# A decoder block's first 26 microseconds: who casts the weights, what is loaded first, and how long TensorE is warmed

## The chip, the cores and the metric

The kernel runs on one core of one Trainium2 chip. The metric is the device time of one execution in microseconds (us). The engines are TensorE (PE in the profile; its weight loads are PEld), VectorE (DVE), ScalarE (ACT), GpSimd (POOL) and SyncE (SP, which here issues most of the DMAs).

## The reference

One layer of a hybrid block on 512 rows of 1024 channels, all in float32. The part that bears on the change is its beginning, the first normalisation and the input projection:

```python
h = rmsnorm(x, norm1_g[l])
z = h @ w_in[l] + b_in[l]                       # 1024 -> 6656 columns
z_glu, z_rx, z_rg, z_ga, z_gb = jnp.split(z, split_idx, axis=-1)
u = z_glu[..., :D_CONV] * jax.nn.sigmoid(z_glu[..., D_CONV:])
...                                             # depthwise convolution, layernorm, silu, projection
...                                             # 4-tap convolution, RG-LRU with block-diagonal gates, projection
m = jax.nn.sigmoid(z_ga) * y_a + jax.nn.sigmoid(z_gb) * y_b
x = x + m @ w_mix_out[l]
h = rmsnorm(x, norm2_g[l])
x = x + (jax.nn.silu(h @ ffn_w1[l]) * (h @ ffn_w3[l])) @ ffn_w2[l]
return rmsnorm(x, norm_f_g)
```

## The kernel before

**How a product is made.** Every float32 operand of a matmul is split in two float32r parts: a high part, which is a cast of the full value, and a low part, the full value minus the high one. `mm3` adds three products per tile of 128 channels: high by high, high (weights) by low (rows), low (weights) by high (rows). With `lo_last=True` all products with the weights' high part come first and those with its low part at the end.

**Weight chunks.** The weights of the projection come in chunks of 1024 x 128 (512 KB), one for each 128 output columns. `emit_chunk` (L140) issues the load on SyncE's queue (L156) into one of `RAW = 4` buffers `raw_in`, and `split_to` (L120) makes the high part `hl_in` with `copy` (L122, on ScalarE, `act.copy`) and the low part on GpSimd (L118, a subtraction of two inputs of 128x1024). `emit_to(n)` emits chunks until n of them are out.

**Small parameters.** Biases, gains and convolution taps are loaded as rows of 128 into tiles `rows` by `load_rows` (L463), one DMA for each of the `parts`, and turned on TensorE into columns by `rows_turned` (L498), from where VectorE copies them into `par` (L499). `row_at` says in which tile and row a parameter lies. Before, norm1_g (8 rows) and b_in (52) share the first tile and are the `first` two parts, the other rows lie in three more tiles.

**The beginning, in an order written out by hand** (L586 to L609, for TensorE, ScalarE, VectorE and SyncE):

- `WARM` float32 matmuls of ones (L486) run on TensorE ahead of everything; each shows as two records in the trace.
- The 512 rows of x lie in four tiles of 128 rows, each in two halves of 512 columns. `norm1_rows(t)` computes two sums of squares on ScalarE (L530, L536) and a square root (L537), a statistic and a reciprocal on VectorE (L531, L538), and scales the rows in place on VectorE (L570).
- `turn_half` turns 256 rows: for each of the 8 blocks of 128 channels two transposes on TensorE (L554), the high part `h1*h` on ScalarE (L557) and the low part `h1*l` on VectorE (L558). The transposes of the second half need banks that the low parts of earlier blocks free.
- `early_mm(i, hf)` multiplies half `hf` of the rows with early chunk i, 24 matmuls of 256 columns (L514). TensorE's order is: warming, first rows turned, first half turned, `early_mm(0, 0)`, `early_mm(1, 0)`, second half turned, `early_mm(2, 0)`, `early_mm(3, 0)`, remaining rows turned, `early_mm(i, 1)` for i = 0 to 3.

SyncE's order before is: x of the first two row tiles, norm1_g, b_in, chunks 0 and 1, x of the last two row tiles, chunk 2, thirteen loads of small rows, chunk 3. After this beginning a planner orders the rest of the kernel (GpSimd's part as well).

Of the kernel before, what the change touches and what calls it, by code (L numbers as in the profile page):

```python
# [13 lines left out]
P = 128  # L14
# [12 lines left out]
ND = D // P  # L27
# [6 lines left out]
RAW = 4  # L34
HL = 5
AHEAD = 4
WARM = 12

FEW, MANY = 32, 112

# [12 lines left out]
ROWS = [  # L53
    ("norm1_g", 8), ("b_in", 52), ("conv_dw_b", 8), ("conv_ln_g", 8), ("conv_ln_b", 8),
    ("conv_b_out", 8), ("lru_conv_b", 10), ("lru_ba", 10), ("lru_bx", 10),
    ("lru_lambda", 10), ("norm2_g", 8), ("lru_conv_w", 40),
    ("conv_dw_w", 248),
]
# [27 lines left out]
def tile_block(ctx, tc, a, out):  # L86
# [15 lines left out]
    def pairt(name, dtype=F32R):  # L102

        return longt(f"{name}h", dtype), longt(f"{name}l", dtype)

    def bank(name):
        return psum.tile([P, T], F32, tag="mm", name=name)

    def bank2(name):
        return psum2.tile([P, T], F32, tag="cv", name=name)  # L110

    vec, act, pe, pool_e = nc.vector, nc.scalar, nc.tensor, nc.gpsimd
# [4 lines left out]
    def sub(eng, o, x, y):  # L117
        return eng.tensor_tensor(out=o, in0=x, in1=y, op=ALU.subtract)  # L118

    def split_to(h, l, full, eng, copy=act.copy):  # L120

        copy(h, full)  # L122
        last = sub(eng, l, full, h.bitcast(F32))
        if eng is pool_e:
            newest["sub"] = last.ins
        return h, l
# [10 lines left out]
    def wchunk(key, src, kt, cols, where="hl", lo=pool_e, after=None):  # L137
        chunks.append((key, src, kt, cols, where, lo, after))

    def emit_chunk():  # L140
        if emitted[0] == GATES_AT:
            load_gates()
        key, src, kt, cols, where, lo, after = chunks[emitted[0]]
        emitted[0] += 1
        n = kt * cols
        if where == "made":
            raw = src()
        else:
            raw = raws.tile([P, 1024], F32, tag="raw", name=f"raw_{key}")
        rv = raw[:, :n]  # L150
        if where == "made":
            pass
        elif callable(src):
            src(raw)
        else:
            newest["load"] = nc.sync.dma_start(rv.rearrange("p (k n) -> p k n", k=kt), src).ins  # L156
        if where != "long":
            hl = hls.tile([P, 2, 1024], F32R, tag="hl", name=f"hl_{key}")
            h, l = split_to(hl[:, 0, :n], hl[:, 1, :n], rv, lo)
            if after:  # L160
                after(rv, h)
            held[key] = (h.rearrange("p (k n) -> p k n", k=kt), l.rearrange("p (k n) -> p k n", k=kt))
        else:
            held[key] = [
                split_to(longt(f"{key}h{i}", F32R), longt(f"{key}l{i}", F32R), rv[:, i * T : (i + 1) * T], lo)
                for i in range(2)
            ]

    def emit_to(n):
        while emitted[0] < min(len(chunks), n):  # L170
            emit_chunk()

    def weights(key, ahead=AHEAD):
        i = next(i for i, c in enumerate(chunks) if c[0] == key)
        emit_to(i + 1 + ahead)
        return held.pop(key)
# [16 lines left out]
    def load_gates():  # L193
      with tc.issue_after(newest["load"]):
        for gi, name in enumerate(("lru_wa", "lru_wx")):
            nc.sync.dma_start(gate_rows[:, gi, :], a[name][0].rearrange("h r n -> (h r) n"))
# [246 lines left out]
    n_rows = sum(n for _, n in ROWS)  # L443
    n_first = ROWS[0][1] + ROWS[1][1]
    par = consts.tile([P, n_rows], F32, name="par")
    row_at = lambda c: (0, c) if c < n_first else (1 + (c - n_first) // P, (c - n_first) % P)
    at, col, parts = 0, {}, []
    for name, n in ROWS:
        col[name] = at
# [10 lines left out]
    def load_rows(i):  # L460
        lo, m, src = parts[i]
        b, r = row_at(lo)
        nc.sync.dma_start(rowt[b][r : r + m, :P], src)  # L463

    x_nat = a["x"].rearrange("b (t p) d -> p (b t) d", p=P)
    xt = [[longt(f"x{t}{h}") for h in range(2)] for t in range(NT)]

    def load_x(t):
        for h in range(2):
            nc.sync.dma_start(xt[t][h], x_nat[:, t, h * T : (h + 1) * T])  # L470
# [13 lines left out]
    wp = bank2("warm")  # L484
    for _ in range(WARM):
        pe.matmul(wp[:, :P], ones, ones, start=True, stop=True)  # L486

    first = [i for i, (lo, _, _) in enumerate(parts) if lo < n_first]
    load_x(0)
    load_x(1)  # L490
    for i in first:
        load_rows(i)

    def rows_turned(c0, c1):
        pt = bank2(f"par_ps{c0}")
        for c in range(c0, c1, P):
            m = min(P, c1 - c)
            pe.transpose(pt[:, c - c0 : c - c0 + m], rowt[row_at(c)[0]][:m, :P], ident[:m, :m])  # L498
        vec.tensor_copy(par[:, c0:c1], pt[:, : c1 - c0])  # L499

    def pc(name, i):
        return par[:, col[name] + i : col[name] + i + 1]


    def mm3(ps, ws, xs, lo_last=False):


        n = 3 * len(ws)
        i = 0
        three = [((wh, xh), (wh, xl), (wl, xh)) for (wh, wl), (xh, xl) in zip(ws, xs)]  # L510
        if lo_last:
            three = [q[:2] for q in three] + [q[2:] for q in three]
        for l, r in (q for qs in three for q in qs):
            pe.matmul(ps, l, r, start=i == 0, stop=i == n - 1)  # L514
            i += 1

    def w_tiles(key, kt, ahead=AHEAD):
        h, l = weights(key, ahead)
        return [(h[:, k, :], l[:, k, :]) for k in range(kt)]
# [21 lines left out]
    def rstd_of(halves, junk, between=None):  # L541
        begun = rstd_begin(halves[0], junk[0])
        if between:
            between()
        return rstd_end(begun, halves[1], junk[1])

    def turn_half(name, rows, gname, dest, hf, bk, some=range(ND)):

        cs = slice(hf * 256, hf * 256 + 256)
        for c in some:  # L550
            ps = bk[c % len(bk)](f"{name}{hf}{c}")
            for t in range(2):
                src = rows[2 * hf + t][c // 4][:, (c % 4) * P : (c % 4 + 1) * P]
                pe.transpose(ps[:, t * P : (t + 1) * P], src, ident)  # L554
            g = pc(gname, c)
            h, l = (v[:, cs] for v in dest[c])
            act.activation(h, ps[:, :256], AF.Copy, scale=g)  # L557
            last = vec.scalar_tensor_tensor(out=l, in0=ps[:, :256], scalar=g, in1=h.bitcast(F32), op0=ALU.mult, op1=ALU.subtract)  # L558
        return last.ins

    def parts_of(pair_tiles, cs=slice(0, T)):
        return [(h[:, cs], l[:, cs]) for h, l in pair_tiles]

    h1p = [pairt(f"h1{c}") for c in range(ND)]

    def norm1_rows(t):
        junk = [shortt(f"n1j{t}{h}") for h in range(2)]
        r = rstd_of(xt[t], junk)
        for h in range(2):
            vec.tensor_scalar(out=xt[t][h], in0=xt[t][h], scalar1=r, scalar2=None, op0=ALU.mult)  # L570
# [6 lines left out]
    def early_mm(i, hf):  # L577
        m = EARLY_IN[i]
        if hf == 0:
            early.append((m, w_tiles(f"in{m}", ND, 0), bank(f"z{m}")))  # L580
        _, ws, ps = early[i]
        mm3(ps[:, HALVES[hf]], ws, parts_of(h1p, HALVES[hf]), lo_last=hf == 0)
# [3 lines left out]
    with tc.manual_schedule(engines={ET.PE, ET.Activation, ET.DVE, ET.SP}):  # L586
        norm1_rows(0)
        norm1_rows(1)
        rows_turned(0, n_first)
        emit_to(1)  # L590
        turn_half("tx", xt, "norm1_g", h1p, 0, [bank, bank, bank, bank2])
        emit_to(2)
        load_x(2)
        load_x(3)
        norm1_rows(2)
        norm1_rows(3)
        emit_to(3)
        for i in range(len(parts)):
            if i not in first:
                load_rows(i)  # L600
        early_mm(0, 0)
        early_mm(1, 0)
        turn_half("tx", xt, "norm1_g", h1p, 1, [bank2, bank, bank])
        emit_to(4)
        early_mm(2, 0)
        early_mm(3, 0)
        rows_turned(n_first, n_rows)
        for i in range(4):
            early_mm(i, 1)  # L609
# [448 lines left out]
    first = {}  # L1058
# [198 lines left out]
```

## Time and profile before

| | |
|---|---|
| time, median of 3 runs | 806.26 us (805.32 to 806.38) |
| profiled execution, its time | 806.61 us |
| profiled execution, span from first to last instruction | 804.8 us |
| mean granted TensorE clock | 0.994 |
| TensorE busy | 791.1 us (98%) |
| VectorE busy | 679.1 us (84%) |
| ScalarE busy | 472.1 us (59%) |
| GpSimd busy | 232.3 us (29%) |

The span lies inside the time of the execution. A busy TensorE is not TensorE at its peak: its matmuls overlap, and the granted clock says at which share of full speed it was let run. In the timeline a row has the start and the length in us, the engine, the line of the code, the operation with the tiles it writes and reads, and how many such instructions in a row were merged; in brackets stands how long the engine had been idle before, and what it waited for.

### The profile page before, as it was taken

What the parts mean: (1) busy time and instruction counts of PE and PEld (TensorE: products, weight loads), DVE (VectorE), ACT (ScalarE), POOL (GpSimd) and SP (SyncE); (2) the same over time, 40 slices, a digit from 0 to 9 for tenths busy, and PEclk for the clock granted to TensorE, in tenths of its full rate; (3) what the DMA queues carried; (4) which work ended last, traced back from release to release, by engine and by line L of the source; (5) the groups of instructions that cost most, each with busy time, mean ns of one, the idle gap of its engine ahead of it and who ended that gap; (6) DMA issues with size and microseconds to landing.
All of it is one profiled execution on the core that took longest, in us unless ns stands there. A gap on an engine that the chain in (4) does not pass through costs nothing.

```text
span 804.8 us, 12198 instructions
## 1 busy us (share of the span) xinstructions
PE 791.1 (98%) x4374; PEld 691.9 (86%) x4374; DVE 679.1 (84%) x1034; ACT 472.1 (59%) x677; POOL 232.3 (29%) x182
## 2 busy tenths in 40 slices
PE   8999999999999999999999999999999999999996
PEld 7988888788888888888888888998999999888885
DVE  5699899999989988787878889977778887899756
ACT  7546585988668855553326474544555555577443
POOL 3575866777766855030000000000000000000000
PEclk9999999999999999999999999999999999999999
DMA  7945646487564764469847545576555543676652
GB/s 214 235 133 152 188 139 208 119 240 204 166 208 140 210 180 119 128 217 273 283 135 236 158 132 157 132 200 166 132 132 132 132 132 105 206 261 200 198 170 104
DMA packets 184625, 140.29 MB, mean 174 GB/s; under 512 B 14280, under 2 KB 162164, under 8 KB 184564
## 3 DMA queue, kind: packets, MB, share of 16 engines
q1 hardware_dynamic: 183123, 134.27, 55.5%
q0 software_dynamic: 1440, 5.24, 3.5%
q8 instruction: 34, 0.56, 0.3%
q14 instruction: 28, 0.22, 0.1%
HBM read 113.79 MB, written 18.64 MB: 165 GB/s over the span
## 4 chain that ended last, share of the span: by engine, by line
PE 83%; DVE 10%; DMA 3%; ACT 2%; issue 1%; POOL 1%; SPq 0%; DVEq 0%; ACTq 0%; POOLq 0%
PE z L514 29%; PE or L926 13%; PE yb L514 7%; PE ft L1053 7%; PE fa L1053 6%; PE ya L514 5%; PE mxr L926 5%; PE fe L1053 3%; DVE cv L673 2%; PE fb L1053 2%; PE g L800 2%; PE fr L1053 2%; DMA raw_fb<-in_ffn_w_dram 1%; PE f L514 1%; DVE hl_ft L118 1%
## 5 line engine op out<-in xcount | busy, mean ns | idle before, releaser
L673 DVE SCALAR_TENSOR_TENSOR cv<-u,par,cv 128x511 f32<-128x511 f32 (+16 forms) x240 | 162.2, 730 | 2.7 <-ACT cv L670 2.5
L118 POOL TENSOR_TENSOR hl_in<-raw_in,hl_in 128x1024 fp32r<-128x1024 f32 x52 | 125.9, 2427 | 80.5 <-ACT hl_in L122 73.0
L344 POOL DMA_DIRECT2D raw_fb<-raw_fb x10 | 8.7, 875 | 303.1 <-DVE raw_fb L346 186.7
L118 POOL TENSOR_TENSOR ows<-ows 128x256 f32<-128x256 f32 x66 | 57.2, 869 | 37.5 <-DMA ows<-in_ffn_w_dram 34.6
L122 ACT CAST hl_in<-raw_in 128x1024 fp32r<-128x1024 f32 x52 | 54.2, 1043 | 9.6 <-PE z L514 6.5
L122 ACT CAST hl_ft<-raw_fb 128x1024 fp32r<-128x1024 f32 x40 | 41.9, 1049 | 29.5 <-DVE raw_fb L346 12.3
L118 DVE TENSOR_TENSOR hl_ft<-raw_fb,hl_ft 128x1024 fp32r<-128x1024 f32 x40 | 48.6, 1219 | 11.2 <-ACT hl_ft L122 11.1
L118 DVE TENSOR_TENSOR hl_fb<-raw_fb,hl_fb 128x1024 fp32r<-128x1024 f32 x30 | 36.6, 1221 | 10.6 <-ACT hl_fb L122 10.4
L514 PE MATMUL z<-h10h,hl_in 128*128 128x512 f32 (+1 forms) x112 | 42.4, 380 | 0.0
L514 PE MATMUL z<-h11h,hl_in 128*128 128x512 f32 (+1 forms) x112 | 41.8, 375 | 0.0
L514 PE MATMUL z<-h13h,hl_in 128*128 128x512 f32 (+1 forms) x112 | 41.8, 375 | 0.0
L514 PE MATMUL z<-h12h,hl_in 128*128 128x512 f32 (+1 forms) x112 | 41.8, 375 | 0.0
L514 PE MATMUL z<-h14h,hl_in 128*128 128x512 f32 (+1 forms) x112 | 41.8, 374 | 0.0
L514 PE MATMUL z<-h16h,hl_in 128*128 128x512 f32 (+1 forms) x112 | 41.7, 374 | 0.0
L514 PE MATMUL z<-h15h,hl_in 128*128 128x512 f32 (+1 forms) x112 | 41.7, 374 | 0.0
L514 PE MATMUL z<-h17h,hl_in 128*128 128x512 f32 (+1 forms) x112 | 41.7, 374 | 0.0
L346 DVE TENSOR_TENSOR raw_fb<-raw_fb,raw_fb 128x1024 f32<-128x1024 f32 x20 | 24.5, 1225 | 17.2 <-DMA raw_fb<-in_ffn_w_dram 16.9
L122 ACT CAST hl_fb<-raw_fb 128x1024 fp32r<-128x1024 f32 x30 | 31.4, 1047 | 6.8 <-PE mxr L926 3.7
L122 ACT CAST hl_ob<-raw_ob 128x1024 fp32r<-128x1024 f32 (+1 forms) x23 | 23.4, 1015 | 20.4 <-PE or L926 11.5
L118 DVE TENSOR_TENSOR hl_ob<-raw_ob,hl_ob 128x1024 fp32r<-128x1024 f32 (+1 forms) x23 | 27.0, 1174 | 9.6 <-ACT hl_ob L122 6.8
L1053 PE MATMUL fe<-hs_0h,hl_ft 128*128 128x256 f32 x160 | 30.8, 284 | 0.4 <-DVE hl_ft L118 0.4
L1053 PE MATMUL ft<-hs_1h,hl_ft 128*128 128x256 f32 x160 | 30.4, 283 | 0.0
(961 smaller groups left out, 2618.9 us busy)
## 6 DMA issues: line engine op xcount, KB each, us to landing
raw_in<-in_w_in_dram SPq DMA_DIRECT2D x52, 512.0 KB
raw_fb<-in_ffn_w_dram SPq DMA_DIRECT2D x96, 256.0 KB
ows<-in_ffn_w_dram SPq DMA_DIRECT2D x44, 256.0 KB
os<-ows SPq DMA_DIRECT2D x22, 512.0 KB
raw_ob<-in_ffn_w_dram SPq DMA_DIRECT2D x33, 256.0 KB
raw_ot<-os SPq DMA_DIRECT2D x33, 256.0 KB
raw_lo<-in_lru_w_out_dram SPq DMA_DIRECT2D x16, 320.0 KB
raw_fb<-raw_fb POOLq DMA_DIRECT2D x10, 512.0 KB, 4.6
```

The costliest lines, as they stand in the source:

```text
L118: return eng.tensor_tensor(out=o, in0=x, in1=y, op=ALU.subtract)
L122: copy(h, full)
L344: pool_e.dma_start(out=q, in_=y, accum_op=ALU.add)
L346: vec.tensor_tensor(out=q, in0=q, in1=y, op=ALU.add)
L514: pe.matmul(ps, l, r, start=i == 0, stop=i == n - 1)
L673: vec.scalar_tensor_tensor(out=acc[c][:, s:], in0=u[c][:, : T - s], scalar=dw(c, s), in1=acc[c][:, s:], op0=ALU.mult, op1=ALU.add)
L800: pe.matmul(ps, l, r, start=k == 0, stop=k == len(mms) - 1)
L926: pe.matmul(banks[i], l_[:, ts], r_, start=start and n == 0, stop=stop and n == 2, skip_group_check=again)
L1053: pe.matmul(ps[:, HALVES[i]], lw[:, 4 * i + c, :], rx_, start=not (again or i or c or m), stop=bool(i and c == 3 and m == 2), skip_group_c ...
```

## The change

The first four chunks' high parts are cast on VectorE (`vec.tensor_copy`) instead of ScalarE. On VectorE's queue the first cast stands behind the copy of norm1_g into `par`, the second between the low parts of blocks 4 and 5 of the first half, the third and fourth ahead of all low parts of the second half. Chunk 3 is loaded right behind chunk 2, ahead of the thirteen small loads. b_in has a tile of rows of its own, is loaded behind x, and is turned with the last rows, one transpose and one copy more. `WARM` goes from 12 to 21. GpSimd's order does not change.

```diff
-WARM = 12
+WARM = 21
...
-    def emit_chunk():
+    def emit_chunk(copy=act.copy):
...
-            h, l = split_to(hl[:, 0, :n], hl[:, 1, :n], rv, lo)
+            h, l = split_to(hl[:, 0, :n], hl[:, 1, :n], rv, lo, copy)
...
-    def emit_to(n):
+    def emit_to(n, copy=act.copy):
         while emitted[0] < min(len(chunks), n):
-            emit_chunk()
+            emit_chunk(copy)
...
-    row_at = lambda c: (0, c) if c < n_first else (1 + (c - n_first) // P, (c - n_first) % P)
+    starts = (0, ROWS[0][1], n_first)
+
+    def row_at(c):
+        b = sum(c >= s_ for s_ in starts) - 1
+        return b + (c - starts[b]) // P, (c - starts[b]) % P
...
-    for i in first:
-        load_rows(i)
+    load_rows(first[0])
...
         norm1_rows(0)
         norm1_rows(1)
-        rows_turned(0, n_first)
-        emit_to(1)
-        turn_half("tx", xt, "norm1_g", h1p, 0, [bank, bank, bank, bank2])
-        emit_to(2)
+        rows_turned(0, ROWS[0][1])
+        emit_to(1, vec.tensor_copy)
+        turn_half("tx", xt, "norm1_g", h1p, 0, [bank, bank, bank, bank2], range(5))
+        emit_to(2, vec.tensor_copy)
+        turn_half("tx", xt, "norm1_g", h1p, 0, [bank, bank, bank, bank2], range(5, ND))
         load_x(2)
         load_x(3)
+        for i in first[1:]:
+            load_rows(i)
         norm1_rows(2)
         norm1_rows(3)
-        emit_to(3)
+        emit_to(4, vec.tensor_copy)
         for i in range(len(parts)):
             if i not in first:
                 load_rows(i)
         early_mm(0, 0)
         early_mm(1, 0)
         turn_half("tx", xt, "norm1_g", h1p, 1, [bank2, bank, bank])
-        emit_to(4)
         early_mm(2, 0)
         early_mm(3, 0)
+        rows_turned(ROWS[0][1], n_first)
         rows_turned(n_first, n_rows)
         for i in range(4):
             early_mm(i, 1)
```

## The prediction

> **What bounds the kernel now.** I read the page first, then the timeline of the first 27 us engine by engine, then the windows view cut at the steps of the granted clock.
>
> ```profile
> span 804.8 us, 12198 instructions
> PE 83%; DVE 10%; DMA 3%; ACT 2%; issue 1%; POOL 1%; SPq 0%; DVEq 0%; ACTq 0%; POOLq 0%
> ```
>
> TensorE is the bound: 83% of the chain that ended last is its work, so a microsecond by which its stream starts sooner shows in the time if nothing later takes it back. The profiled execution took 806.61 us, 1.81 us more than its span, and lies 0.35 us above the median of 806.26. A measurement of this kernel can tell about 0.2% (1.6 us) from no change. The first 26 us on TensorE:
>
> ```profile
> 1.09 5.33 PE L486 MATMUL warm<-ones 128*128 128x128 f32 x24 [1.09 <-DVE ones L479]
> 7.48 0.24 PE L498 MATMUL par_ps<-ident,rows 60*128 60x60 f32 x1 [1.06 <-DMA rows<-in_b_in_dram]
> 8.66 2.67 PE L554 MATMUL tx<-ident,x 128*128 128x128 f32 x15 [0.68 <-DVE x L570]
> 10.98 0.56 PE L514 MATMUL z<-h10h,hl_in 128*128 128x256 f32 x1
> 13.73 0.28 PE L514 MATMUL z<-h17l,hl_in 128*128 128x256 f32 x1
> 14.80 0.28 PE L514 MATMUL z<-h10h,hl_in 128*128 128x256 f32 x1
> 17.68 2.49 PE L554 MATMUL tx<-ident,x 128*128 128x128 f32 x16
> 20.12 0.39 PE L514 MATMUL z<-h10h,hl_in 128*128 128x256 f32 x1
> 26.07 0.48 PE L498 MATMUL par_ps<-ident,rows 128*128 128x128 f32 x3
> 26.32 0.36 PE L514 MATMUL z<-h10h,hl_in 128*128 128x256 f32 x1
> ```
>
> A row is start, length, instruction, count. The row at 14.80 begins the second early weight chunk, the rows at 17.68 are the second half's transposes, the row at 20.12 begins the third chunk, and from 26.32 the stream runs on. So I carry four checkpoints through the change: 14.80, 17.68, 20.12 and 26.32.
>
> ```profile
> 2.71:6.12 3.41, 3.41 (x18) 3.41 (x17) 0.78 (x4) 1.83 (x6) 0.00 (x0) 1.00 0.95 321
> 6.12:9.53 3.41, 1.67 (x13) 1.25 (x12) 1.75 (x7) 2.54 (x6) 0.00 (x0) 1.00 1.12 301
> 9.53:12.95 3.42, 3.42 (x19) 3.42 (x17) 2.88 (x8) 3.42 (x10) 2.38 (x1) 0.50 1.02 338
> 12.95:16.36 3.41, 3.41 (x30) 3.41 (x30) 1.71 (x5) 3.34 (x10) 2.41 (x1) 1.00 0.30 75
> 16.36:19.77 3.41, 3.41 (x28) 2.79 (x26) 2.42 (x8) 2.71 (x7) 1.60 (x1) 1.00 0.52 131
> ```
>
> After the stretch come busy times of PE, PEld, DVE, ACT and POOL, then granted clock, DMA share and GB/s. TensorE was busy for only 1.67 of the 3.41 us from 6.12, and the next 3.42 us had clock 0.50. (Before 6.12 the trace has no clock record, and the view fills in 1.00; the warming matmuls take 5.33 / 24 = 0.22 us each, so I take them to have run at half clock.)
>
> **The change, part by part.** *More warming.* 21 instructions instead of 12 make 42 records instead of 24. The 18 new ones start at 6.42. At full clock I put them at half of 0.22, 0.11 us, together 2.0, so they end at 8.4; if the clock does not rise, at 18 x 0.22 = 4.0, so 10.4. I take the first, since the full stretch 2.71 to 6.12 was busy and the record says 1.00 from 6.12. Behind them queues the transpose of norm1_g (0.24 us), then the first transposes of x, which waited for VectorE's scaled rows until 8.66 anyway. 8.4 + 0.24 is under 8.66: no cost. The other end costs 10.4 + 0.24 - 8.66 = 2.0 us at the start. In exchange the stretch 6.12 to 9.53 is busy but for some 0.3 us, and the 0.50 after it goes. On TensorE alone that is worth: about eight transposes and ten matmuls at half speed, 1.7 us of a 3.42 us stretch. Whether it arrives depends on who feeds these matmuls:
>
> ```profile
> 8.62 1.05 ACT L122 CAST hl_in<-raw_in 128x1024 fp32r<-128x1024 f32 x1 [0.73 <-DMA raw_in<-in_w_in_dram]
> 9.58 0.47 ACT L557 ACTIVATE h10h<-tx,par 128x256 fp32r<-128x256 f32 x1
> 12.08 0.52 ACT L557 ACTIVATE h17h<-tx,par 128x256 fp32r<-128x256 f32 x1
> 8.12 0.88 DVE L570 TENSOR_SCALAR x<-x,stats 128x512 f32<-128x512 f32 x2
> 8.91 0.21 DVE L499 COPY par<-par_ps 128x60 f32<-128x60 f32 x1
> 10.07 0.48 DVE L558 SCALAR_TENSOR_TENSOR h10l<-tx,par,h10h 128x256 fp32r<-128x256 f32 x1 [0.95 <-ACT h10h L557]
> 12.83 0.47 DVE L558 SCALAR_TENSOR_TENSOR h17l<-tx,par,h17h 128x256 fp32r<-128x256 f32 x1
> 9.75 2.38 POOL L118 TENSOR_TENSOR hl_in<-raw_in,hl_in 128x1024 fp32r<-128x1024 f32 x1 [8.44 <-ACT hl_in L122]
> ```
>
> ScalarE makes the eight high halves every (12.08 - 9.58) / 7 = 0.36 us, VectorE the low ones every (12.83 - 10.07) / 7 = 0.39. Two full-clock matmuls take 0.24 ((17.68 - 14.80) / 24 = 0.12 each). So at full clock the stream waits for VectorE, and h17l, ending 13.30, sets when the first chunk can pass on.
>
> *Casts on VectorE.* The first takes ScalarE's 1.05 us away from in front of h10h, which then starts behind the copy of par, at about 9.1 instead of 9.58. But VectorE gets four casts in its queue: one ahead of h10l, one between h14l and h15l, two ahead of the second half's low parts. The price of one, and what it may wait for:
>
> ```profile
> 54.26 0.28 DVE L214 CAST hl_gate<-raw_gate 32x256 fp32r<-32x256 f32 x1 [0.53 <-POOL hl_gate L118]
> 227.86 0.73 POOL L118 TENSOR_TENSOR ows<-ows 128x256 f32<-128x256 f32 x1
> 227.94 0.81 DVE L214 CAST hl_gate<-raw_gate 32x256 fp32r<-32x256 f32 x1 [0.57 <-POOL hl_gate L118]
> 13.61 2.41 POOL L118 TENSOR_TENSOR hl_in<-raw_in,hl_in 128x1024 fp32r<-128x1024 f32 x1 [1.48 <-ACT hl_in L122]
> 15.32 1.37 DVE L570 TENSOR_SCALAR x<-x,stats 128x512 f32<-128x512 f32 x2
> 17.38 0.88 DVE L570 TENSOR_SCALAR x<-x,stats 128x512 f32<-128x512 f32 x2
> ```
>
> A cast of 256 columns takes 0.28 us, a one-input operation of 512 takes 0.88 / 2 = 0.44: 0.16 per 256 more, so 0.28 + 3 x 0.16 = 0.76 for 1024; 0.7 to 0.76, I take 0.7. The upper bound is a two-input operation's rate, 1.2 us. And such a cast stands still while GpSimd runs a subtraction: the one at 227.94 took 0.81 and ended 0.16 us after GpSimd's (228.59); the pair at 15.32 took 1.37 instead of 0.88, across the end of GpSimd's at 16.02. The small-operand operations h10l to h17l don't wait: they kept 0.39 us through GpSimd's 9.75 to 12.13.
>
> So, in VectorE's order: par copied by 9.1; cast 0 from 9.0 to 9.7; h10l at 9.65 and on every 0.39, h14l ending 11.7. GpSimd's subtraction 0 starts 0.08 us after its cast (9.75 against 9.67 before), at 9.78, and ends at 12.16. Cast 1, due at 11.6, stands until then and needs 4 x 0.16 = 0.6 more: 12.75. Then h15l, h16l, h17l end at 13.15, 13.55 and 13.95, where before h17l ended at 13.30. The last low matmul goes at 14.0 instead of 13.73, and the checkpoint 14.80 moves to **15.0**, 17.68 to **17.9**: 0.2 us later, although the clock was full. Here the 1.7 us end: TensorE waits for VectorE, and VectorE for GpSimd.
>
> ```profile
> 18.29 0.48 ACT L557 ACTIVATE h10h<-tx,par 128x256 fp32r<-128x256 f32 x1 [0.20 <-PE tx L554]
> 18.80 0.48 DVE L558 SCALAR_TENSOR_TENSOR h10l<-tx,par,h10h 128x256 fp32r<-128x256 f32 x1 [0.54 <-ACT h10h L557]
> 17.12 2.52 SPq L156 DMA_DIRECT2D raw_in<-in_w_in_dram  x3
> 13.38 0.69 ACT L530 ACTIVATE n1j<-x 128x512 f32<-128x512 f32 x1
> 14.80 0.29 ACT L537 ACTIVATE stats<-stats 128x1 f32<-128x1 f32 x1
> 22.56 4.75 POOL L118 TENSOR_TENSOR hl_in<-raw_in,hl_in 128x1024 fp32r<-128x1024 f32 x2 [2.02 <-ACT hl_in L122]
> ```
>
> The second half takes these 0.2 us back. Before, TensorE's first pair of transposes waited for x's last rows, scaled at 17.38 to 18.26, and h10h followed at 18.29. After, these scalings start sooner, since ScalarE's squares no longer queue behind a cast (13.38 before, about 12.1 after): the square root follows the statistic at about 14.0 instead of 14.80, the first pair stands behind subtraction 1 (12.8 to 15.2) and ends at 15.9, the second at 17.4. The transposes at 17.9 find all rows there, and h10h comes two transposes later, at about 18.3 as before. Cast 2 runs from 17.3 to 18.0 and cast 3 at its heels to 18.7, just ahead of h10l at 18.8. Checkpoint 20.12 stays at **20.1**. GpSimd then does subtractions 2 and 3 from 18.7 to 23.5, where the fourth chunk's ended at 22.56 + 4.75 / 2 = 24.9; the third chunk's low part is due 16 x 0.12 = 1.9 us after 20.1, at 22.0, the fourth's at 24.9: both hidden, the second at 0.1 to 0.2 us less than before (20.12 to 26.07 is 5.95 for 48 matmuls worth 5.76).
>
> *Fourth chunk earlier.* Its load moves from 17.12 to about 9, past thirteen small loads on SyncE's queue. From 12.95 to 16.36 DMA was 0.30 busy, so the queue had drained at about 14.0; 512 KB more at 338 GB/s take 1.55 us: landed at about 15.6 to 16.6, ahead of cast 3 at 17.9. The small rows land some 1.5 us later, at most near 20, and are due at 26.
>
> *b_in's rows later.* 26 KB less ahead of the first chunk: 0.1 us, hidden behind VectorE. One transpose more (0.48 / 3 = 0.16) in front of 26.32, and one copy of 0.21 in front of par's second. Sum at 26.32: -0.2 + 0.16, so 0 (from -0.3 to +0.3). From there on the orders of instructions on all engines are the same, and I find nothing to make it larger: the time stays at 806.6 for a profile like this, **806.3** as a median.
>
> **The rivals.** *VectorE's casts don't wait for GpSimd* (chance 0.10): then h17l ends at 13.45, the checkpoints move to 14.55 and 17.45, h10h to 17.85: -0.45, so 805.8. Against it stands the cast at 227.94. Even ScalarE's own pace (h17h ending at 12.1) leaves no more than 1.2 us to win.
>
> *The clock falls again* (0.18). TensorE will be fed at 0.24 in 0.39 us from 10.3 and stand idle from 12.0 to 13.2 behind cast 1. If that stretch counts as idle, 3.41 us at 0.50 follow at about 13 to 16.4, of which 2.4 us hold dense matmuls: +1.2, so 807.5. Two rows tell what counts:
>
> ```profile
> 16.36:19.77 3.41, 1.49 (x13) 1.28 (x11) 1.00 0.52 131
> 555.67:559.08 3.41, 1.53 (x13) 1.36 (x12) 2.64 (x3) 0.72 (x2) 0.00 (x0) 1.00 0.97 275
> 559.08:562.49 3.41, 3.41 (x18) 3.41 (x17) 2.68 (x4) 2.58 (x4) 0.00 (x0) 0.50 0.53 154
> ```
>
> The first is the same view for line L514 alone: 1.49 us of matmuls and otherwise transposes, and the clock stayed at 1.00, while 1.53 us of 3.41 at 555.67 were followed by 0.50. So transposes seem to count, and the stretch from 9.53, with transposes to 10.3, would be about two thirds busy. The Trainium skill ("TensorE: Matmul & The Clock Gate", Part 4: PE-mode transpose) says the opposite, that a transpose doesn't count as TensorE being busy; by that rule this rival would be the likely one. The same page (Part 1) has the windows run free of the kernel's start; no run here shows it yet, and it would make the clock's steps differ between executions.
>
> *Cast 3 loses to GpSimd* (0.08): slower. If the fourth chunk lands after about 18.0, or cast 3 starts later than 0.08 us after cast 2, GpSimd begins subtraction 2 first, and cast 3 waits to 20.4 and ends at 21.0. The second half's low parts queue behind it, the last transposes wait for h10l to free a bank, and 20.1 becomes 22.3: +2.2, so 808.5. For it: nothing holds GpSimd back but that order. Against: VectorE's next operation starts before its last has ended (8.91 against 9.00), and the chunk has 1 to 2 us in hand.
>
> *The warming runs into the rows* (0.05), the bound above at half clock: part of 2.0 is swallowed as above, +1, so 807.3.
>
> **How the numbers follow.** Forecast 0.57 (806.3), the rivals 0.10, 0.18, 0.08 and 0.05, and 0.02 for the rest. Medians shown spread over 1.1 us, so the low end is 805.8 less 0.8, 805.0; the high end takes in the clock with 0.7 more, 808.2. No case reaches 1.6 us of gain but by chance: faster 0.06. Slower takes the lost order and part of the two at +1: 0.18. Same 0.76.
>
> **What would show it.** Right: granted clock 1.00 from about 6 us; h10h at 9.1; cast 1 on VectorE over 1 us long and ending 0.6 after GpSimd's subtraction; TensorE idle from 12.0 to 13.2; 15.0, 17.9, 20.1 and 26.3 at the checkpoints. Wrong: a cast 1 of 0.7 us; clock 0.50 from about 13; cast 3 longer than 1 us; or a shift between 26 us and the end that the checkpoint at 26.3 doesn't have.

## Result, and the profile after

The changed kernel takes 804.56 us (median of 14, 803.73 to 805.51), the kernel before, run beside it, 806.32 us (median of 14, 805.13 to 808.09). The ratio is 0.9971 with a 95% interval of 0.9961 to 0.998: about 0.3% faster, where 806.3 and no change were forecast. The profiled execution of the changed kernel took 804.1 us, 1.8 us more than its span. From its page: span and busy rows, the queues' row on instructions, and the chain that ended last.

```profile
span 802.3 us, 12234 instructions
PE 790.7 (99%) x4393; PEld 691.6 (86%) x4393; DVE 681.2 (85%) x1039; ACT 467.8 (58%) x673; POOL 232.3 (29%) x182
q8 instruction: 34, 0.56, 0.3%
PE 79%; DVE 11%; DMA 5%; ACT 2%; issue 2%; POOL 1%; SPq 0%; DVEq 0%; POOLq 0%; ACTq 0%
```

TensorE is the bound as before. It has 4393 instructions and as many weight loads, 4374 each before: 38 more, 36 of them from the warming, 2 from b_in's own transpose. The timeline of TensorE over the first 27 us (start, length, line, operation; the changed kernel's line numbers are 4 to 7 higher):

```profile
1.09 7.11 PE L491 MATMUL warm<-ones 128*128 128x128 f32 x42 [1.09 <-DVE ones L484]
8.90 1.86 PE L558 MATMUL tx<-ident,x 128*128 128x128 f32 x15 [0.28 <-DVE x L574]
13.38 0.39 PE L518 MATMUL z<-h15l,hl_in 128*128 128x256 f32 x1 [0.85 <-DVE h15l L562]
15.32 0.28 PE L518 MATMUL z<-h10h,hl_in 128*128 128x256 f32 x1
18.20 2.29 PE L558 MATMUL tx<-ident,x 128*128 128x128 f32 x16
20.45 0.38 PE L518 MATMUL z<-h10h,hl_in 128*128 128x256 f32 x1
26.88 0.36 PE L518 MATMUL z<-h10h,hl_in 128*128 128x256 f32 x1
```

The four checkpoints stand at 15.32, 18.20, 20.45 and 26.88: 0.52, 0.52, 0.33 and 0.56 us *later* than before. The clock did become full, as the windows view shows (PEclk, the granted clock, is the third number from the end):

```profile
6.12:9.53 3.41, 3.13 (x27) 2.80 (x26) 2.47 (x9) 1.82 (x6) 0.00 (x0) 1.00 1.12 311
9.53:12.95 3.42, 2.99 (x23) 2.50 (x21) 3.42 (x8) 3.42 (x11) 2.38 (x1) 1.00 1.08 360
12.95:16.36 3.41, 2.98 (x22) 2.80 (x23) 2.73 (x8) 2.35 (x10) 2.39 (x1) 1.00 1.04 251
```

So a kernel whose beginning ends half a microsecond later ends 2.5 us earlier (span 804.8 to 802.3). To find where, I followed the same instructions down both timelines. Before, TensorE late in the kernel:

```profile
516.21 0.50 PE L1053 MATMUL fe<-hs_0h,hl_ft 128*128 128x256 f32 x2 [0.42 <-DVE hl_ft L118]
558.41 0.36 PE L1053 MATMUL ft<-h24h,hl_ft 128*128 128x256 f32 x1 [1.88 <-DVE se L879]
```

The same two instructions after:

```profile
516.71 0.50 PE L1060 MATMUL fe<-hs_0h,hl_ft 128*128 128x256 f32 x2 [0.36 <-DVE hl_ft L118]
557.29 0.35 PE L1060 MATMUL ft<-h24h,hl_ft 128*128 128x256 f32 x1 [0.25 <-DVE se L886]
```

At 516 us the changed kernel is still 0.50 late, at 558 it is 1.12 early: 1.62 us are made in between, and 1.88 - 0.25 = 1.63 is what the one stop in front of `ft` lost. The rest follows at once. Before, the half clock of the windows 555.67 and 559.08 (shown in the prediction) came behind that stop; after, these windows read:

```profile
555.67:559.08 3.41, 3.16 (x27) 2.99 (x26) 2.94 (x4) 1.84 (x4) 0.00 (x0) 1.00 0.74 203
559.08:562.49 3.41, 3.41 (x30) 3.41 (x30) 3.11 (x3) 2.74 (x4) 0.00 (x0) 1.00 0.54 159
```

30 matmuls instead of 18 in 559.08 to 562.49: the other 1.4 us. Not every execution of the kernel before has that half clock (run 1 below has the stop without it), and the medians differ by 1.8 us, not by 2.5. Outside this stretch the distance between the two streams hardly changes: the same matmuls are 0.54 to 0.56 us late from 28 to 430 us, 0.50 at 545, and 2.5 to 2.6 early from 567 us to the end.

What holds TensorE there? Backwards from `ft`: VectorE's `se`, behind VectorE's sum `raw_fb` (L346), behind a load of `raw_fb`, which SyncE issues only when GpSimd's accumulating transfer (L344, a DMA that adds one weight tile into another) is done with the buffer. Before, in the timeline of GpSimd and VectorE, and in the waits of SyncE's queue from 544 to 560 us (total, times, longest):

```profile
546.70 0.86 POOL L344 DMA_DIRECT2D raw_fb<-raw_fb  x1 [13.82 <-DVE raw_fb L346]
556.44 1.23 DVE L346 TENSOR_TENSOR raw_fb<-raw_fb,raw_fb 128x1024 f32<-128x1024 f32 x1 [3.89 <-DMA raw_fb<-in_ffn_w_dram]
```

```profile
SPq L334 <- DMA raw_fb<-raw_fb: 7.4, 1, 7.4
```

And in the DMA view of before, cut to 547.7 to 548.0 us, and then to 546 to 553 (the transfer's last number is us from issue to landing):

```profile
q8 instruction: 1, 0.02, 31.6%
...
raw_fb<-raw_fb POOLq DMA_DIRECT2D x1, 512.0 KB, 5.5
```

After, the same timeline:

```profile
546.69 0.86 POOL L344 DMA_DIRECT2D raw_fb<-raw_fb  x1 [13.37 <-DVE raw_fb L346]
555.32 1.23 DVE L346 TENSOR_TENSOR raw_fb<-raw_fb,raw_fb 128x1024 f32<-128x1024 f32 x1 [2.77 <-DMA raw_fb<-in_ffn_w_dram]
```

And the same cuts of the DMA view after, the first at 546.8 to 547.0:

```profile
q8 instruction: 1, 0.02, 33.2%
...
raw_fb<-raw_fb POOLq DMA_DIRECT2D x1, 512.0 KB, 4.5
```

The transfer is issued at the same moment in both, 546.70 and 546.69, and lands 1.0 us earlier after; VectorE's sum comes 1.12 us earlier. What differs is one packet of 16 KB on the queue q8, named "instruction": before, it starts at 547.77, 1.08 us behind the issue, and takes 1.51 us; after, at 546.82, 0.13 us behind it, and takes 1.06. The page of before gives 34 such packets too, for 4374 + 4374 instructions of TensorE and its weight loads, one for 257. The Trainium skill ("Runtime: NRT & Kernel Launch", Instruction fetch mechanics) says that each engine streams its instructions in blocks of 16 KiB, 256 instructions, over a DMA queue of its own, and that this is mostly hidden. The count agrees.

That gave the **fetch theory**: the gain has nothing to do with a warmer or an earlier beginning. The added instructions of TensorE shift, in the whole rest of the program, the moments at which its next block is fetched, and the one near 547 us slips out of a transfer that the path was waiting for. Its rival, the **beginning theory**: the full clock of the first 13 us is carried to the end by a path that the checkpoints don't show.

### The profile page after: what moved, and what is told of

Its sections match the earlier page's. It is cut to its first block, busy times and chain, and to the rows that moved or that the text cites. A ratio compares the mean times of both kernels' runs of the same rounds, so it can differ in the third digit from the quotient of the medians.

```text
span 802.3 us, 12234 instructions
## 1 busy us (share of the span) xinstructions
PE 790.7 (99%) x4393; PEld 691.6 (86%) x4393; DVE 681.2 (85%) x1039; ACT 467.8 (58%) x673; POOL 232.3 (29%) x182
## 4 chain that ended last, share of the span: by engine, by line
PE 79%; DVE 11%; DMA 5%; ACT 2%; issue 2%; POOL 1%; SPq 0%; DVEq 0%; POOLq 0%; ACTq 0%
PE z L518 29%; PE or L933 13%; PE yb L518 7%; PE fa L1060 6%; PE ft L1060 5%; PE ya L518 5%; PE mxr L933 5%; DVE cv L680 2%; PE fb L1060 2%; PE fe L1060 2%; DMA raw_fb<-in_ffn_w_dram 2%; PE g L807 2%; DMA raw_fb<-raw_fb 2%; DVE raw_fb L346 1%; DVE hl_ft L118 1%
## 5 line engine op out<-in xcount | busy, mean ns | idle before, releaser
L344 POOL DMA_DIRECT2D raw_fb<-raw_fb x10 | 8.7, 874 | 299.9 <-DVE raw_fb L346 186.2
L122 ACT CAST hl_in<-raw_in 128x1024 fp32r<-128x1024 f32 x48 | 50.0, 1042 | 9.8 <-PE z L518 6.6
L346 DVE TENSOR_TENSOR raw_fb<-raw_fb,raw_fb 128x1024 f32<-128x1024 f32 x20 | 24.5, 1224 | 17.2 <-DMA raw_fb<-in_ffn_w_dram 16.9
```

The costliest lines, as they stand in the source:

```text
L344: pool_e.dma_start(out=q, in_=y, accum_op=ALU.add)
L346: vec.tensor_tensor(out=q, in0=q, in1=y, op=ALU.add)
```

## The experiments

Each run has the kernel before beside it on the same chip. "Stop" is TensorE's idle time in front of the `ft` near 558 us, "landing" the transfer's time from issue to landing near 547 us (and "landing near 532" that of the transfer before it), "fetch over" the end of q8's packet counted from the issue near 547 us; these four are of the one profiled execution of each run.

| run | more TensorE instructions | fetch over at | landing | landing near 532 | stop | median us | ratio (95%) |
|---|---|---|---|---|---|---|---|
| before (its profile) | 0 | +2.59 | 5.5 | 4.9 | 1.88 | 806.32 |  |
| changed (its profile) | 38 | +1.19 | 4.5 | 4.5 | 0.25 | 804.56 | 0.9971 (0.9961 to 0.998) |
| 1 before again | 0 | +1.42 | 5.2 | 6.0 | 2.21 | 806.93 | 0.9991 (0.9978 to 1.0004) |
| 2 changed again | 38 | +1.54 | 5.7 | 4.5 | 1.69 | 804.77 | 0.9964 (0.9952 to 0.9977) |
| 3 warming alone | 36 | +1.19 | 4.5 | 4.5 | 0.33 | 804.49 | 0.9958 (0.9944 to 0.9972) |
| 4 all but the warming | 2 | +2.28 | 5.2 | 4.9 | 1.63 | 808.25 | 1.0009 (0.9996 to 1.0022) |
| 5 21 small warming matmuls | 36 | +1.10 | 4.5 | 4.5 | 0.20 | 804.38 | 0.9973 (0.996 to 0.9985) |
| 6 224 columns | 0 | +1.46 | 5.4 | 5.6 | 2.45 | 806.62 | 1.0003 (0.9991 to 1.0015) |
| 7 26 warming matmuls | 56 | -0.05 | 4.5 | 4.5 | 0.57 | 804.55 | 0.9969 (0.9956 to 0.9982) |
| 8 4 warming matmuls | -32 | +5.61 | 5.2 | 6.0 | 2.32 | 809.26 | 1.0029 (1.0013 to 1.0044) |
| 9 176 columns | 0 | +1.35 | 4.9 | 6.0 | 2.35 | 807.7 | 1.0014 (1.0003 to 1.0025) |
| 10 nearly a whole block | 240 | +3.30 | 6.2 | 5.0 | 2.83 | 808.55 | 1.0017 (1.0005 to 1.0029) |
| 11 casts on ScalarE | 38 | +1.38 | 5.0 | 4.5 | 1.02 | 805.29 | 0.9978 (0.9969 to 0.9988) |
| 12 addition on VectorE | 0 | no transfer |  | 5.7 | 0.20 | 804.71 | 0.9977 (0.9967 to 0.9987) |
| 13 176 columns, x on time | 0 | +1.66 | 5.2 | 5.4 | 1.89 | 806.65 | 0.9996 (0.9986 to 1.0007) |
| 14 addition and 26 | 56 | no transfer |  | 4.5 | none | 804.24 | 0.9968 (0.9958 to 0.9979) |
| 15 two additions and 26 | 56 | no transfer |  | no transfer | none | 804.15 | 0.9969 (0.9958 to 0.998) |

The last transfer before it, near 532 us, counts too: SyncE's next loads go 0.05 us behind its landing, and VectorE's sums ahead of the issue near 547 us wait for them. In runs 1, 6, 8, 9 and 13 it landed 0.9 to 1.5 us later than the 4.5 of the changed kernel, and the transfer near 547 us was then issued 15.15 to 15.93 us behind it instead of 14.23. So the stop follows the lateness of both transfers and not of the second alone: run 9, with a landing of only 4.9 near 547 us, stops for 2.35.

**Runs 1 to 4: which part of the change.** Made before the fetch was seen; their expectations hold the theories of that moment. Runs 1 and 2 are the two kernels unedited. Run 3 is the kernel before with one line changed, run 4 the changed kernel with that line back:

```diff
-WARM = 12
+WARM = 21
```

> The kernel before, unchanged, so that its stops can be seen in a second profiled execution. Theory L (late): in the two profiles the beginning is no gain (TensorE +0.50 us at the checkpoint 26.07) and all of the difference arises at one stop, 556.54 to 558.41 (1.88 us idle, behind a load that waits for GpSimd's accumulating transfer) and in the clock stretch of 0.50 from 559.08 behind it; then this execution stops there again for over 1 us. Theory N (noise of the pair): the stop was an accident of that execution, 5.22 us for a transfer that elsewhere takes 4.2; then this execution stops there for about 0.3 us as the changed kernel did, and its time is about 805.2 or lower. Theory E (early): in most executions the beginning of the kernel before is later than in the profile shown, because the clock's steps fall elsewhere; then checkpoint 26.07 is later than 26.5.

> The changed kernel, unchanged, in a second profiled execution. Theory L: no stop over 0.5 us at about 557 and no clock under 1.00 between 10 and 790 us. Theory N: the stop comes and goes in both kernels. Theory E: its beginning repeats within 0.2 us (26.6 at the checkpoint), since no cold stretch is in it. Time about 804.6 under all three.

> The kernel before with 21 instead of 12 warming instructions and nothing else. Theory E: the whole gain, about 804.7. Theory L, if what matters at 557 is where the beginning puts the rest: unclear, between 804.5 and 806.3. The prediction's reckoning: first half limited by the low parts (h17l at 13.3), second half by x's last rows, so the checkpoint 17.68 at about 17.4, 20.12 unchanged, 806.2.

> The changed kernel with 12 instead of 21 warming instructions. Theory E: the gain is gone, 806 or more; the beginning is later by up to 1.7 us, with a stretch of clock 0.50 after about 9.5. The prediction's reckoning: matmuls wait for the low parts anyhow, at most +0.3. Theory L or N: about 804.6, the beginning being swallowed.

The difference repeats (806.93 against 804.77). The warming alone has all of it (804.49), and casts, order of loads and b_in's rows without the warming have none (1.0009). Yet run 3's beginning is no earlier than before's: its fourth checkpoint stands at 26.31, before's at 26.32.

Run 1 alone did not decide between the theories. It has the stop of theory L (2.21) and also the late beginning of theory E. TensorE's timeline has a wait there for the fourth chunk's low part, which the first profile of before doesn't have:

```profile
25.74 0.38 PE L514 MATMUL z<-h10h,hl_in 128*128 128x256 f32 x1 [0.31 <-POOL hl_in L118]
```

The fourth checkpoint of one and the same kernel thus lies at 26.32 in one execution and at 27.04 in another (run 1), 0.72 us apart, more than the 0.56 by which the changed kernel is later. Against run 1, run 3's beginning is 0.73 us earlier, of the 2.7 us between their spans (804.7 and 802.0). Run 2's profiled execution, the slowest of its six with 805.89, shows the stop of 1.69 with the transfer at 5.7, although it is the changed kernel: there the packet came 0.17 us behind the issue and took longer than in the first profile (1.36 against 1.06 us). Theory L had expected no such stop in run 2. So the changed kernel stands at the edge and can fall off.

**Runs 5 to 8: instructions or time.** Run 5 has the changed kernel's number of warming instructions in the old warming's time, run 6 the reverse:

```diff
-WARM = 12
+WARM = 21
-        pe.matmul(wp[:, :P], ones, ones, start=True, stop=True)
+        pe.matmul(wp[:64, :73], ones[:, :64], ones[:, :73], start=True, stop=True)
```

```diff
+    wide = longt("wide")
+    vec.memset(wide[:, :224], 1.0)
-        pe.matmul(wp[:, :P], ones, ones, start=True, stop=True)
+        pe.matmul(wp[:, :224], ones, wide[:, :224], start=True, stop=True)
```

Runs 7 and 8 are the kernel before with `WARM = 26` and `WARM = 4`.

> The kernel before, with the changed kernel's 21 warming matmuls instead of 12, but each of 64 rows by 73 columns instead of 128 by 128, so that the warming takes about as long as before (to about 6.4 us) and TensorE has the changed kernel's 36 instructions more. Fetch theory (the gain is made near 547 us, where a 16 KB packet of the queue q8, one for each 257 instructions of TensorE, no longer falls into GpSimd's accumulating transfer): the clock falls to 0.50 at about 9 as before and the checkpoint at 26.3 does not move, but the transfer ends 4.2 us after its issue, TensorE's stop near 557 is 0.2 to 0.4 us, and the time is 804.3 to 804.9. Beginning theory (the gain comes from the full clock in the first 13 us, carried by some path to the end): the clock falls at 9, so no gain, 806.0 to 807.5.

> The kernel before, with 12 warming matmuls as there, but each over 224 columns instead of 128, so that TensorE is warmed as long as with 21 and has not one instruction more. Fetch theory: clock 1.00 through the first 13 us, yet the packet falls into the transfer near 547 us as before, the transfer ends 4.9 to 5.3 us after its issue, TensorE's stop near 557 is 1.5 to 2.2 us, and the time is 806.0 to 807.5. Beginning theory: the whole gain, 804.3 to 804.9, with a stop of 0.2 to 0.4.

> The kernel before with 26 warming matmuls: 56 instructions of TensorE more than before, 20 more than in the changed kernel. Fetch theory: the packet near 547 us comes another 0.8 to 1.2 us earlier in the program than with 21, ahead of the transfer's issue; the stop near 557 is at most 0.4 us in every execution and the time is 804.2 to 804.8, so that the executions lie at least as close together as with 21. Beginning theory: nothing more is to be had by it, and if the longer warming (to about 9.3) runs into the rows, it loses 0.3 to 0.7 against 21: 804.7 to 805.3.

> The kernel before with 4 warming matmuls: 32 instructions of TensorE fewer than before. Fetch theory: the packet near 547 us comes about 1.9 us later, some 3 us after the transfer's issue, still inside it; the transfer ends 4.6 to 5.3 us after its issue, the stop is 1 to 2 us, and the time is 806.0 to 808.5, the half clock of the beginning, which falls elsewhere, included. Beginning theory: a colder beginning, slower than before by 0.5 to 2 us, all of it visible at the checkpoint at 26.3.

Run 5's windows, and then its timeline of TensorE:

```profile
9.53:12.95 3.42, 3.42 (x18) 3.42 (x17) 2.92 (x8) 3.42 (x10) 2.38 (x1) 0.51 1.08 362
```

```profile
1.09 5.25 PE L486 MATMUL warm<-ones 128*64 128x73 f32 x42 [1.09 <-DVE ones L479]
557.03 0.36 PE L1053 MATMUL ft<-h24h,hl_ft 128*128 128x256 f32 x1 [0.20 <-DVE se L879]
```

The half clock of the beginning is all there, and so is the whole gain: 804.38. This is what the beginning theory could not give. Run 6 kept the stop of before (2.45, a little over the 2.2 expected) and its time, but it proves little by its time: the tile for the wide columns took a buffer that x needed, the first rows came at 6.16 instead of 3.67 us, and the stream began 1.7 us late. Run 7 lies at 804.55, as expected, with a stop slightly over the 0.4 expected (0.57). Run 8 is slower than before, and its time (809.26) and its stop (2.32) lie over the ranges expected; 0.9 us of the time is lost by the fourth checkpoint, at 27.23. Its packet missed the expectation's place (4.7 us behind the issue instead of 3). Transfers further up, at 519 and 534 us, had already been hit (they ended 0.8 and 1.4 us later than undisturbed), and the issues behind them came 14.91 and 15.83 us apart instead of 14.00 and 14.23 in the changed kernel. The transfer landed at 5.2 all the same, with a packet that began only as its own last ones ended; why, the records don't tell.

**Runs 9 to 12: the wait taken away, and the beginning.** Run 9 is run 6 with 176 columns. Run 10 has 72 tiny warming matmuls, 240 instructions more:

```diff
-WARM = 12
+WARM = 72
-        pe.matmul(wp[:, :P], ones, ones, start=True, stop=True)
+        pe.matmul(wp[:32, :16], ones[:, :32], ones[:, :16], start=True, stop=True)
```

Run 11 is the changed kernel with `emit_to(1)`, `emit_to(2)` and `emit_to(4)` in their places without `vec.tensor_copy`. Run 12 is the kernel before with VectorE doing the sum of the transfer near 547 us:

```diff
-        elif n == "t4" or k in ADDING:
+        elif (n == "t4" and k != 4) or k in ADDING:
             pool_e.dma_start(out=q, in_=y, accum_op=ALU.add)
```

> As the run with 224 columns, which ran into the first rows and began the stream over 1 us late: 12 warming matmuls, here over 176 columns, so that they end near 8 us, ahead of the rows, and TensorE has not one instruction more than before. Fetch theory: clock 1.00 through the first 13 us and the checkpoint at 26.3 within 0.3 us, yet the packet of q8 near 547 us falls into the accumulating transfer, which ends 4.5 to 5.4 us after its issue; the stop near 557 is 1.4 to 2.4 us and the time 806.0 to 807.5. Beginning theory: 804.3 to 804.9, with a stop of 0.2 to 0.6.

> The kernel before with 72 warming matmuls of 32 rows by 16 columns: 240 instructions of TensorE more, all but 17 of a whole packet of 257. Fetch theory: the packets are one ahead in count and stand in the program where they stood before, about 1 us later (17 instructions at 17 a microsecond): the packet near 547 us comes 1.0 to 2.1 us after the transfer's issue, the transfer ends 4.5 to 5.4 us after it, the stop is 1.4 to 2.4 us and the time is 806.0 to 808.0. If more warming instructions were good in themselves, whatever the packets, the gain of 36 would stay: 804.3 to 805.0. The beginning itself should be within 0.5 us of before, if the small matmuls take under 0.05 us each.

> The changed kernel with its first four casts on ScalarE again; order of loads, b_in's rows and warming stay changed. This parts the 0.3 to 0.6 us by which the changed kernel's checkpoints lie later than before's and than those of the kernel before with 21 warming matmuls. If the casts on VectorE, one standing still behind GpSimd's subtraction, are the cause (the prediction's step): the checkpoint at 26.3 comes at 26.2 to 26.5. If the order of the loads is: it stays at 26.8 to 27.2. The time is 804.3 to 805.0 by the fetch theory either way, since the number of TensorE's instructions is the changed kernel's.

> The kernel before, with the one accumulating transfer at 547 us taken away: the same sum is made by VectorE (one more addition of 1024 columns, about 1.22 us), so that the load of raw_fb behind it waits for no transfer; TensorE's instructions, the beginning and the packets of q8 stay as before. Fetch theory: the stop of TensorE near 557 falls from 1.9 us to at most 0.6, unless VectorE's longer queue makes a new one, and the time goes to 804.0 to 805.2 with the old beginning. Beginning theory: the stop there is not what cost the time, 806.0 to 808.0.

Run 12's timeline of VectorE and TensorE:

```profile
549.28 1.22 DVE L346 TENSOR_TENSOR raw_fb<-raw_fb,raw_fb 128x1024 f32<-128x1024 f32 x1
557.64 0.35 PE L1053 MATMUL ft<-h24h,hl_ft 128*128 128x256 f32 x1 [0.20 <-DVE se L879]
```

The addition that replaces the transfer is the first row; the stop is gone, and with the old warming the kernel takes 804.71. In this execution the clock happened not to fall in the beginning; the windows view:

```profile
9.53:12.95 3.42, 3.32 (x21) 2.57 (x19) 3.22 (x8) 3.42 (x9) 2.25 (x1) 1.00 1.09 358
```

Its fourth checkpoint, at 26.48, is no earlier than before's for that. Run 12 by itself therefore does not part the stop from the clock; runs 5 and 13 do.

Run 10's timeline of TensorE, and then its DMA view:

```profile
1.09 7.86 PE L486 MATMUL warm<-ones 128*32 128x16 f32 x144 [1.09 <-DVE ones L479]
560.63 0.36 PE L1053 MATMUL ft<-h24h,hl_ft 128*128 128x256 f32 x1 [2.83 <-DVE se L879]
```

```profile
raw_fb<-raw_fb POOLq DMA_DIRECT2D x1, 512.0 KB, 6.2
```

With nearly a whole block of 257 added, the packet is back inside the transfer, and q8 has 35 packets instead of 34. The stop (2.83), the landing (6.2) and the time (808.55) all lie over the ranges expected. Part of the time is lost in the beginning: the small matmuls took 7.86 us (0.055 each, not under 0.05), and the fourth checkpoint came at 26.89, 0.57 later than before's. More warming instructions are not good in themselves. Run 9 had its rows late again (6.29 us) and its clock at 0.50 from 10.3, and its time (807.7) lies over the range of both theories, so it tells nothing that run 13 doesn't. Run 11 missed both expectations: the fourth checkpoint came at 27.56, later than with the casts on VectorE (26.88). Left in the places that the change gives them, between block 4 and block 5, the casts cost more on ScalarE, where h15h waited behind a cast of 1.08 us. So the run shows that these places are no better on ScalarE; it does not part VectorE's casts from the order of the loads, and what the changed kernel's beginning loses, if anything, stays open. Its packet ended 1.38 us behind the issue, the transfer took 5.0, and its median of 805.29 lies in between like its stop.

**Runs 13 to 15: the cell still missing, and whether gains add.** Run 13 lends the 176 columns from a weight buffer, so that x is on time; run 14 joins runs 7 and 12; run 15 also replaces the transfer near 532 us:

```diff
+    wide = raws.tile([P, 1024], F32, tag="raw", name="wide")
+    vec.memset(wide[:, :176], 1.0)
-        pe.matmul(wp[:, :P], ones, ones, start=True, stop=True)
+        pe.matmul(wp[:, :176], ones, wide[:, :176], start=True, stop=True)
```

```diff
-        elif n == "t4" or k in ADDING:
+        elif (n == "t4" and k not in (3, 4)) or k in ADDING:
```

> 12 warming matmuls over 176 columns again, with the columns in one of the buffers of the weight chunks, so that the loads of x are not held up as they were in the two runs before (6.2 us for the first rows instead of 3.7): a warming to about 8 us with not one instruction of TensorE more. Fetch theory: no clock of 0.50 at 9 and the checkpoint at 26.3 within 0.4 us, but the packet near 547 us falls into the transfer, which ends 4.5 to 5.4 us after its issue; stop near 557 of 1.4 to 2.4 us; 805.8 to 807.5. Beginning theory (clock in the first 13 us): the whole gain, 804.3 to 804.9, stop of 0.2 to 0.6.

> Both remedies together: 26 warming matmuls, and the sum of the transfer near 547 us made by VectorE. Fetch theory: they remove the same stop, so their gains do not add: 804.0 to 804.8, the stop near 557 at most 0.3 us, and the executions no wider apart than 1.5 us. If they were two causes, the gains would add: 802.0 to 803.0.

> As the run with one addition on VectorE and 26 warming matmuls, with the transfer near 532 us replaced by an addition on VectorE too. Fetch theory: with 26 the packet near 532 lies ahead of that transfer already, so nothing is left to win: 803.9 to 804.8; VectorE's 1.22 us more could cost up to 0.5 where it is late.

Run 13's windows, and then its timeline of TensorE:

```profile
6.12:9.53 3.41, 2.09 (x15) 1.60 (x15) 1.45 (x6) 2.45 (x7) 0.00 (x0) 1.00 1.10 308
9.53:12.95 3.42, 3.26 (x22) 2.56 (x20) 2.96 (x8) 3.42 (x10) 2.38 (x1) 1.00 1.09 362
```

```profile
26.32 0.36 PE L516 MATMUL z<-h10h,hl_in 128*128 128x256 f32 x1
558.60 0.36 PE L1055 MATMUL ft<-h24h,hl_ft 128*128 128x256 f32 x1 [1.89 <-DVE se L881]
```

Full clock, the same checkpoint 26.32 as before, no instruction more: 806.65, no gain, and the stop of 1.89. With it the square of four is full. Medians with the old instruction count are 806.3 to 807.7 (the runs of before beside these) at the old warming and 806.65 with the longer one; with 36 instructions more they are 804.38 at the old warming time (run 5) and 804.49 at the longer (run 3). Where the clock fell is known for the profiled executions alone, and these say the same. With the stop they took 806.61 (half clock, before) and 805.41 (full clock, run 13); without it 803.72 (half clock, run 5) and 803.84 (full clock, run 3). The count decides, the clock of the beginning does not. Runs 14 and 15 do not add up (804.24 and 804.15 where two causes would have given 802 to 803): warming and addition remove the same stop. They are the lowest of all, but their ratios (0.9968 and 0.9969) are those of the changed kernel within the intervals. Run 14's executions lie closest together, 803.69 to 804.73.

## Why the prediction was wrong

**The step that failed** is the last of the sum: "From there on the orders of instructions on all engines are the same, and I find nothing to make it larger". That put the stretch from 26 us to the end at nothing. The orders were the same in both profiles; the moments of the instruction fetches were not, and in the profiled executions they turned a kernel 0.50 us late at 516 us into one 2.5 us early at the end. The prediction priced the 18 added records by the time that they take at the start and nowhere counted the instructions, though the page's row `q8 instruction: 34` lists what carries them. The row at 555.67 that I used as evidence on the clock was itself the mark of the stop that went: I read it for its clock and never asked what TensorE waited for there. The prediction's own last sign, "a shift between 26 us and the end that the checkpoint at 26.3 doesn't have", is what came.

**Warming** was right: 42 records, 7.11 us long, ending at 8.20 where 8.4 was forecast, the clock at 1.00 from 5.66 us on, and the 1.7 us of full clock did not arrive at the checkpoints (run 13: 26.32 against 26.32).

**The casts** were right in size and cause; the rows of VectorE, ScalarE and GpSimd after:

```profile
9.23 0.68 DVE L122 CAST hl_in<-raw_in 128x1024 fp32r<-128x1024 f32 x1
11.88 1.05 DVE L122 CAST hl_in<-raw_in 128x1024 fp32r<-128x1024 f32 x1
17.56 1.29 DVE L122 CAST hl_in<-raw_in 128x1024 fp32r<-128x1024 f32 x2
9.41 0.47 ACT L561 ACTIVATE h10h<-tx,par 128x256 fp32r<-128x256 f32 x1 [1.28 <-DVE par L503]
10.00 2.38 POOL L118 TENSOR_TENSOR hl_in<-raw_in,hl_in 128x1024 fp32r<-128x1024 f32 x1 [8.69 <-DVE hl_in L122]
18.32 5.12 POOL L118 TENSOR_TENSOR hl_in<-raw_in,hl_in 128x1024 fp32r<-128x1024 f32 x2 [2.92 <-DMA rows<-in_lru_lambda_dram]
```

A cast takes 0.68 (0.7 forecast). ScalarE's h10h comes at 9.41 (9.1 forecast), behind x's rows, whose second pair VectorE scaled from 8.36 instead of 8.12 on. Cast 1 stands until GpSimd's subtraction ends at 12.38 and needs 0.55 more (0.6 forecast), TensorE is idle for 0.85 us behind it (1.2 forecast), and casts 2 and 3 both begin ahead of GpSimd's next subtraction (cast 3 at 18.16, the subtraction at 18.32), so the rivals "don't wait" and "cast 3 loses" are out. The clock did not fall again either (1.00 in the windows to 16.36); by the Trainium skill's sentence on transposes ("TensorE: Matmul & The Clock Gate", Part 4) that rival was likely, and here it did not come.

**The checkpoints** came 0.3 to 0.6 us later than the forecast 15.0, 17.9, 20.1 and 26.3. From the first rows on the working, which forecast no change, holds within 0.3: the row of 15 transposes started at 8.90 instead of 8.66, and from there to the fourth checkpoint it is 26.88 - 8.90 = 17.98, against 26.32 - 8.66 = 17.66 before, and 26.31 - 8.29 = 18.02 in run 3, which has only the warming. Part of it is the start of the rows, which differs between executions; the fourth checkpoint of before alone differs by 0.72 (run 1). In two other executions the rival "the warming runs into the rows" came true by a few tenths. Warming and transposes in run 2, then in run 3:

```profile
1.09 7.57 PE L491 MATMUL warm<-ones 128*128 128x128 f32 x42 [1.09 <-DVE ones L484]
8.74 2.32 PE L558 MATMUL tx<-ident,x 128*128 128x128 f32 x16
```

```profile
1.09 6.38 PE L486 MATMUL warm<-ones 128*128 128x128 f32 x42 [1.09 <-DVE ones L479]
8.29 1.86 PE L554 MATMUL tx<-ident,x 128*128 128x128 f32 x15 [0.36 <-DVE x L570]
```

The same 42 records take 6.38 to 7.64 us (the longest in run 11), as the clock rose at 4.1 to 6.75 us, and in run 2 the transposes follow the warming without a pause. This is what the Trainium skill ("TensorE: Matmul & The Clock Gate", Part 1) says of the clock's windows, that they run free of the kernel's start; the runs agree. Little of this reaches the end: run 3 and the changed kernel differ by 0.57 us at 26 us and by 0.3 in the span.

## What to carry to other kernels

An edit that adds instructions moves every later instruction fetch of that engine; where a path waits for a transfer, look whether a packet of the "instruction" queue lies on it before giving a far-off gain or loss to the edit's purpose. A gain that appears hundreds of microseconds behind an edit asks for two controls: the same instruction count without the edit's effect, and the effect with the old count. Better than hitting a lucky count is to take the fragile wait away (run 12), which doesn't depend on it.

## What the runs showed of the hardware

The fetch of TensorE's next 16 KB (0.9 to 2.1 us a packet in these executions) holds up an accumulating transfer of 512 KB if it is still under way about when the transfer's own packets begin. Undisturbed, these move from 1.43 to 4.2 us behind the issue. Over the 166 such transfers of the 17 profiled executions: wherever the fetch began no more than 2 us ahead of the issue and was over by +1.19 us (37 times), or none was near (72 times), the last packet ended at +4.19 to +4.36; wherever it began before +2.2 and ended at +1.31 or later (27 times), at +4.59 to +6.13, without an exception either way. In the other 30 the packet began at +4.30 or later, when the transfer was over or nearly so, and the end was +4.19 to +4.68. The Trainium skill's word that a fetch is mostly hidden ("Runtime: NRT & Kernel Launch", Instruction fetch mechanics) is true of TensorE itself here (the packet at 546.82 us in the profile after lies in an unbroken stream of matmuls), and not of the transfer beside it. Which of the 16 DMA engines carries the packet the records don't tell, so that it is one late engine that holds the whole transfer is argued and not shown. A late transfer costs only where a path waits: in runs 7, 14 and 15 the transfer near 605 us ended at +5.7 to +6.13, and TensorE did not stop.
